# One mixture-of-experts kernel: thirteen larger experts do gate and up with the weights standing on the array, and the last expert's blocks go together

## The chip, the cores and the metric

The kernel runs on one core of one Trainium2 chip. The time is device microseconds (us) from the first to the last instruction of one launch, plus what little lies around it; the median of several launches counts. Engines are called by their short names: PE (matrix products), ACT (activations and copies), DVE (vector operations), POOL (here mostly indirect transfers), SP (issues the plain transfers). PEclk in the rows is the share of its full clock that PE was granted.

## The reference, cut to what matters

One layer on a sequence of tokens of 1,024 features: a normalised mLSTM branch and a pooling branch, an output product, and then a hierarchical mixture of 32 experts, each with gate, up and down matrices of 1024x512, 1024x512 and 512x1024. Each token goes to two experts; the last step is a norm over the whole output. The change is in the mixture and in the last norm.

```python
g_idx = argmax(hf @ w_rg + b_rg)                 # one of 4 groups
top_val, top_loc = lax.top_k(e_logits_of_that_group, 2)
gates = softmax(top_val) * g_gate
# for every expert e, over the tokens routed to it:
a = xb @ w_gate[e]
b = xb @ w_up[e]
out = (silu(a) * b) @ w_down[e]
y[token] += out * gate
x = x + gate_f * y
return rms_norm(x, final_g)
```

## The kernel before, in words

**Order of experts.** The experts are counted, ranked by size and taken in 32 positions (the loop variable `e`). Position 31, the last, holds the largest expert. Positions 3, 7 and 11 hold ranks 1 to 3; 13, 15, 17, 19, 21, 23, 25, 27 and 29 hold ranks 4 to 12. All other positions hold small experts of at most 128 tokens. So from position 12 on the positions alternate: an even one with one block of 128 rows (a single expert), an odd one with a larger expert.

**Products.** Everything is float32 in three passes: each operand is split into a high and a low part (`ehi`, `elo` for weights, `xh`, `xl` for the tokens), and a product is hi*xh + hi*xl + lo*xh. The weights of one expert come in 12 pieces of 128x1024; for each, ACT makes `ehi` (L143) and DVE makes `elo` (L144), one expert ahead of its use. The generator `feed` hands out these splits, and `take(n)` at named places (the hooks "gate", "silu", "up0", ...) puts n pieces into the instruction streams there. The engines work in the order in which the program is written.

**A single expert** (`core`, class `Block`). The tokens' rows are fetched by an indirect transfer on POOL (`gather`, tile `xg`, from `h2d`), turned by PE (`pxt`), split into `xh` and `xl`, and stand on the array; the weights stream through: 24 matmuls of 512 columns for gate (`pg`), 48 of 256 columns for up (`pu`), then 4 transposes of the activation (`pat`) and 24 matmuls of 512 columns for down (`py`). DVE weighs the result into `y` (L326) and POOL adds it to `acc` in DRAM with an indirect transfer (L334), one after the other.

**A larger expert** (`joint_core`). At ranks 1 to 3 it does two whole blocks, at ranks 4 to 12 one block and one half block of 64 rows (class `Half`), whose `xh` and `xl` stand side by side on the array, so that it needs two passes instead of three. In both, tokens stand and weights stream.

**Buffers.** The half block's turned activation `ahl` lies in the buffer `wraw1`, which the gather of the next larger expert's second block also uses: that gather waits for the last down product that reads `ahl`. `y` of a single and the first block's `y` share one buffer (tag `y`), which comes free when the scatter has landed.

**The last expert** (position 31). Its three blocks go one after the other (`core` for two, and for the third `half_core` or `core`, by a branch on the count). While they run, hooks fetch the 16 row tiles of `acc` (SP, L1749), square them on ACT (L1756), take the roots on DVE (L1760 and L135 to L139) and scale them on DVE (L1768) or on ACT and POOL (L1765, L1766).

Of the kernel before, what the change touches and what calls it, by code (L numbers as in the profile page):

```python
# [18 lines left out]
P = 128  # L19
T = 2048  # L20
# [19 lines left out]
SR = P // 2  # L40
N_FULL, N_HALF = 4, 9
# [12 lines left out]
def body(ctx, tc, x, c, ada_w, ada_b, norm1_g, w_in, conv_w, conv_b, w_q, w_k, b_igate, b_fgate,  # L54
# [46 lines left out]
    def full_at(q):  # L101
        return q == 0 or rank_at[q] < N_FULL

    def half_at(q):
        return N_FULL <= rank_at[q] < N_FULL + N_HALF
# [17 lines left out]
    cnt_p = const.tile([1, NE], I32, name="cnt_p")  # L123
# [23 lines left out]
    class Tiles:  # L147
# [5 lines left out]
        of_tag.update({t: 1 for t in ("xh", "xl", "act", "ah", "al", *(f"{a}2{q}" for a in ("ehi", "elo") for q in range(4)))})  # L153
# [70 lines left out]
    def gather(e, b, n=P):  # L224
        if e >= NE:
            return

        xg = xgs[e, 1] if b == 2 else hx.tile([P, D], F32, name="xg", tag=f"wraw{b}") if e or b else \
            wb.tile([P, D], F32, name="xg", tag="elo03")
        r = T if e or b else T - CH  # L230
        at = bass.IndirectOffsetOnAxis(ap=at_of(gix, gix_0, e, b)[0:n], axis=0)
        gathers.append(keep(G.indirect_dma_start(out=xg[0:n], out_offset=None, in_=h2d[0:r, :], bounds_check=r - 1,  # L232
                                                 oob_is_err=False, in_offset=at)))
        xgs[e, b] = xg

    def gather_further(e):

        if e < NE and full_at(e):
            gather(e, 1)
        elif e < NE and half_at(e):  # L240
            gather(e, 1, SR)

    def x_t(e, b):
        xg = xgs[e, b]
        n = "" if b == 0 else "i"
        xh = wb.tile([P, KT, P], F32R, name="xh" + n, bufs=1)
        xl = wb.tile([P, KT, P], F32R, name="xl" + n, bufs=1)
# [23 lines left out]
    class Block:  # L271


        def __init__(self, e, b, x, beside=False):
            self.e, self.b, self.x = e, b, x
            self.n = "i" if beside else ""
            self.pg = None

            self.y = wb.tile([P, D], F32, name="y", tag="yi") if beside else None
            self.a = self.y[:, 512:1024] if beside else wb.tile([P, DE], F32, name="act")  # L280
            self.ah = wb.tile([P, 4, P], F32R, name="ah", tag="ah" + self.n)
            self.al = wb.tile([P, 4, P], F32R, name="al", tag="al" + self.n)
            self.pus, self.py = {}, {}

        def turn_x(self, i):
            if i == 0:
                self.x = x_t(self.e, self.b)

        def gate(self, k0=0, k1=KT):
            if k0 == 0:  # L290
                self.pg = ps.tile([P, DE], F32, name="pg", tag="py0" if self.n else "pg", bufs=1)
            mm_all(self.pg, *self.x, lambda k: [t_[:, k % 2, :] for t_ in units[self.e, 0, k // 2]], k0, k1)
# [4 lines left out]
        def up(self, h, k0=0, k1=KT):  # L297
            if k0 == 0:
                self.pus[h] = ps.tile([P, 256], F32, name="pu", bufs=2)
            cs = slice(h * 256, h * 256 + 256)  # L300
            mm_all(self.pus[h], *self.x, lambda k: [t_[:, k % 2, cs] for t_ in units[self.e, 1, k // 2]], k0, k1)

        def gated(self, h):
            cs = slice(h * 256, h * 256 + 256)
            keep(V.tensor_tensor(self.a[:, cs], self.a[:, cs], self.pus[h], op=OP.mult))

        def turn(self, h):
            p_ = ps.tile([P, 2, P], F32, name="pat", bufs=1)
# [13 lines left out]
        def weigh(self, hf):  # L322
            if self.y is None:
                self.y = wb.tile([P, D], F32, name="y", tag="y" if self.e or self.b else "xh")
# [12 lines left out]
    class Half:  # L337
# [3 lines left out]
        def __init__(self, e, b, at, within):  # L341
            self.e, self.b, self.at, self.within = e, b, at, within
            self.xs = wb.tile([P, KT, P], F32R, name="xs", tag="xhi", bufs=1)
            self.y = wb.tile([SR, D], F32, name="ys", tag="xli", bufs=1)

            self.a = self.y[:, 512:1024]
            self.pus, self.py, self.as_ = {}, {}, None

        def turn_x(self, i):
            p_ = ps.tile([P, 4, SR], F32, name="pxs", tag="pxt", bufs=2)  # L350
            for j in range(4):
                PE.transpose(p_[:, j, :], xgs[self.e, self.b][0:SR, i * 4 + j::KT], ident[0:SR, 0:SR])
            s = slice(i * 4, i * 4 + 4)
            keep(S.activation(self.xs[:, s, 0:SR], p_, AF.Copy))
            keep(V.tensor_tensor(self.xs[:, s, SR:P], p_, self.xs[:, s, 0:SR].bitcast(F32), op=OP.subtract))

        def mm2(self, out_, a, bh, bl, first, last):
            PE.matmul(out_, a, bh, start=first, stop=False)
            PE.matmul(out_, a, bl, start=False, stop=last)

        def added(self, out_, p_):

            keep(S.activation(out_, p_[SR:P, :], AF.Copy))
            keep(V.tensor_tensor(out_, p_[0:SR, :], out_, op=OP.add))

        def gate(self):
            self.pg = ps.tile([P, DE], F32, name="pgs", tag="py0", bufs=1)
            for k in range(KT):
                hi, lo = units[self.e, 0, k // 2]
                self.mm2(self.pg, self.xs[:, k, :], hi[:, k % 2, :], lo[:, k % 2, :], k == 0, k == KT - 1)  # L370

        def silu(self):
            for h in range(2):
                cs = slice(h * 256, h * 256 + 256)
                self.added(self.a[:, cs], self.pg[:, cs])
            for h in range(2):
                cs = slice(h * 256, h * 256 + 256)
                keep(S.activation(self.a[:, cs], self.a[:, cs], AF.Silu))

        def up(self, h, k0=0, k1=KT):  # L380
            if k0 == 0:
                self.pus[h] = ps.tile([P, 256], F32, name="pu", bufs=2)
            cs = slice(h * 256, h * 256 + 256)
            for k in range(k0, k1):
                hi, lo = units[self.e, 1, k // 2]
                self.mm2(self.pus[h], self.xs[:, k, :], hi[:, k % 2, cs], lo[:, k % 2, cs], k == 0, k == KT - 1)

        def gated(self, h):
            cs = slice(h * 256, h * 256 + 256)
            t_ = self.y[:, cs]  # L390
            self.added(t_, self.pus[h])
            keep(V.tensor_tensor(self.a[:, cs], self.a[:, cs], t_, op=OP.mult))

        def turn(self, h):
            if self.as_ is None:
                self.as_ = wb.tile([P, 4, P], F32R, name="ahl", tag="ah", bufs=1) if self.within else \
                    hx.tile([P, 4, P], F32R, name="ahl", tag="wraw1")
            p_ = ps.tile([P, 2, SR], F32, name="pas", tag="pat", bufs=1)
            for j in range(2):
                PE.transpose(p_[:, j, :], self.a[:, (2 * h + j) * P:(2 * h + j + 1) * P], ident[0:SR, 0:SR])  # L400
            s = slice(2 * h, 2 * h + 2)
            keep(S.activation(self.as_[:, s, 0:SR], p_, AF.Copy))
            keep(V.tensor_tensor(self.as_[:, s, SR:P], p_, self.as_[:, s, 0:SR].bitcast(F32), op=OP.subtract))

        def down(self, k, hf):
            if hf not in self.py:
                self.py[hf] = ps.tile([P, 512], F32, name="pys", tag=f"py{hf}", bufs=1)
            hi, lo = units[self.e, 2, k]
            cs = slice(hf * 512, hf * 512 + 512)
            self.mm2(self.py[hf], self.as_[:, k, :], hi[:, 0, cs], lo[:, 0, cs], k == 0, k == 3)  # L410

        def weigh(self, hf):
            cs = slice(hf * 512, hf * 512 + 512)
            self.added(self.y[:, cs], self.py[hf])
            keep(V.scalar_tensor_tensor(self.y[:, cs], self.y[:, cs], gts[self.b][0:SR, self.e:self.e + 1],
                                        gate_f[0:SR, cs], op0=OP.mult, op1=OP.mult))

        def add(self):
            keep(G.indirect_dma_start(out=acc[:, :], in_=self.y, in_offset=None, bounds_check=T - 1, oob_is_err=False,
                                      out_offset=bass.IndirectOffsetOnAxis(ap=self.at[0:SR, self.e:self.e + 1], axis=0),  # L420
                                      compute_op=OP.add))

    def core(e, b, x, after=lambda m: None):
# [7 lines left out]
        A.gated(0)  # L431
# [4 lines left out]
        A.gated(1)  # L436
# [13 lines left out]
        if e < NE - 1:  # L450
            A.add()
        return A.y

    def half_core(e, b, after=lambda m: None):
        H = Half(e, b, six[b], True)
        for i in range(2):
            H.turn_x(i)
        H.gate()
        after("silu")
        H.silu()  # L460
# [1627 lines left out]
```

## Time and profile before

| | |
|---|---|
| time, median of 3 launches | 1662.3 us (1659.3 to 1669.67) |
| the profiled execution | 1654.61 us, span 1652.9 us |
| mean granted PE clock over the span | 0.978 |
| PE busy | 1558.2 us, 94% |
| DVE busy | 1381.8 us, 84% |
| ACT busy | 931.6 us, 56% |
| POOL busy | 272.9 us, 17% |

The profile is one execution. "Busy" counts an engine as busy from an instruction's start to its modelled end, so matmuls that overlap show longer ends than their spacing; the spacing of starts is what a stream of matmuls costs. The experts take the second half of the span, from 822 us on.

### The profile page before, as it was taken

How to read it: one execution, taken by the hardware profiler on the slowest of the kernel's cores; microseconds unless marked ns; L12 is line 12 of the kernel's file. 1: busy time of each engine (PE TensorE's matmuls, PEld its weight loads, DVE VectorE, ACT ScalarE, POOL GpSimd, SP SyncE). 2: the span in 40 equal slices, each digit the busy share in tenths (PEclk: the TensorE clock that was granted, in tenths of full speed). 3: DMA queues.
4: the chain of work that ended last, by engine and by line, in shares of the span. 5: the costliest groups of instructions: out<-in, count | busy, mean ns of one | idle time of the engine just before them, and what ended most of it. 6: DMA issues, size and time to landing. Idle time of an engine off the chain costs nothing. (4 is left out here: it accounts for less than half of the span.)

```text
span 1652.9 us, 25544 instructions
## 1 busy us (share of the span) xinstructions
PE 1558.2 (94%) x8865; PEld 1327.9 (80%) x8865; DVE 1381.8 (84%) x2754; ACT 931.6 (56%) x1501; POOL 272.9 (17%) x172
## 2 busy tenths in 40 slices
PE   3989999999999999999799999999999999999984
PEld 3868887877978788877688888888888888888873
DVE  6889877997789779988877887968889888899867
ACT  4246554655365554655366665746666666666653
POOL 0000000003020001000233331322123222132134
PEclk7999999999999999999999999999999999999997
DMA  8973276323652345345779898988898888898684
GB/s 306 320 253 103 81 240 202 126 63 105 240 113 76 103 153 159 85 155 197 266 249 358 297 383 269 390 262 283 306 338 292 292 283 294 309 337 314 222 294 198
DMA packets 143463, 384.94 MB, mean 233 GB/s; under 512 B 17220, under 2 KB 68459, under 8 KB 126942
## 3 DMA queue, kind: packets, MB, share of 16 engines
q1 hardware_dynamic: 124374, 340.95, 57.9%
q0 software_dynamic: 13920, 40.79, 9.8%
q10 hardware_dynamic: 5032, 1.51, 0.4%
q8 instruction: 71, 1.16, 0.3%
q14 instruction: 66, 0.54, 0.1%
HBM read 340.61 MB, written 48.08 MB: 235 GB/s over the span
## 5 line engine op out<-in xcount | busy, mean ns | idle before, releaser
L144 DVE TENSOR_TENSOR elo<-eraw,ehi 128x1024 fp32r<-128x1024 f32 x384 | 452.9, 1215 | 33.8 <-ACT ehi L143 26.5
L143 ACT ACTIVATE ehi<-eraw 128x1024 fp32r<-128x1024 f32 x384 | 382.1, 1054 | 19.4 <-PE py L260 7.8
L143 ACT ACTIVATE whi<-wraw 128x1024 fp32r<-128x1024 f32 (+1 forms) x100 | 105.8, 1058 | 146.0 <-PE big L260 52.4
L258 PE MATMUL big<-hh,whi 128*128 128x512 f32 x384 | 157.9, 411 | 0.7 <-DVE v L854 0.7
L260 PE MATMUL big<-hh,wlo 128*128 128x512 f32 x384 | 153.0, 399 | 2.0 <-DVE wlo L144 2.0
L259 PE MATMUL big<-hl,whi 128*128 128x512 f32 x384 | 153.7, 400 | 0.0
L334 POOL DMA_INDIRECT acc<-y,six x35 | 119.6, 3418 | 166.7 <-DVE y L326 141.5
L144 DVE TENSOR_TENSOR wlo<-wraw,whi 128x1024 fp32r<-128x1024 f32 (+1 forms) x100 | 122.2, 1222 | 20.4 <-ACT whi L143 19.1
L266 PE MATMUL pu<-ehi,xh 128*128 128x256 f32 x496 | 125.1, 286 | 0.0
L232 POOL DMA_INDIRECT xg<-h2d,gix x47 | 62.6, 1331 | 375.1 <-PE pxt L251 295.7
L267 PE MATMUL pu<-ehi,xl 128*128 128x256 f32 x496 | 123.8, 284 | 0.0
L258 PE MATMUL py<-ehi,ah 128*128 128x512 f32 x288 | 118.3, 411 | 4.1 <-ACT ah L312 4.1
L259 PE MATMUL py<-elo,ah 128*128 128x512 f32 x288 | 113.4, 394 | 0.0
L260 PE MATMUL py<-ehi,al 128*128 128x512 f32 x288 | 113.2, 395 | 0.0
L260 PE MATMUL big<-whi,yl 128*128 128x512 f32 x256 | 100.6, 408 | 8.0 <-DVE yl L144 7.8
L258 PE MATMUL big<-whi,yh 128*128 128x512 f32 x256 | 105.5, 413 | 1.4 <-ACT yh L143 1.2
L259 PE MATMUL big<-wlo,yh 128*128 128x512 f32 x256 | 102.3, 400 | 0.0
L266 PE MATMUL pg<-ehi,xh 128*128 128x512 f32 x248 | 98.2, 396 | 0.0
L1349 POOL DMA_INDIRECT table<-pay,si x28 | 37.2, 1329 | 363.2 <-DVE si L1344 210.8
L267 PE MATMUL pg<-ehi,xl 128*128 128x512 f32 x248 | 96.8, 390 | 0.0
L267 PEld LDWEIGHTS pu<-ehi,xl 128*128 128x128 f32 x496 | 94.9, 191 | 1.2
L266 PEld LDWEIGHTS pu<-ehi,xh 128*128 128x128 f32 x496 | 94.8, 191 | 1.3
(489 smaller groups left out, 3908.1 us busy)
## 6 DMA issues: line engine op xcount, KB each, us to landing
eraw<-in_w_expert_gate_dram SPq DMA_DIRECT2D x64, 1024.0 KB
eraw<-in_w_expert_up_dram SPq DMA_DIRECT2D x64, 1024.0 KB
eraw<-in_w_expert_down_dram SPq DMA_DIRECT2D x128, 512.0 KB, 7.4
wraw<-in_w_in_dram SPq DMA_DIRECT2D x64, 512.0 KB, 3.7
adaw<-in_ada_w_dram SPq DMA_DIRECT2D x40, 512.0 KB, 4.5
wraw<-in_w_out_dram SPq DMA_DIRECT2D x36, 512.0 KB, 4.1
xq<-in_x_dram SPq DMA_DIRECT2D x16, 512.0 KB, 6.3
bcs<-mad SPq DMA_DIRECT2D x16, 512.0 KB, 6.2
```

Source lines behind the costliest of these rows:

```text
L143: i = S.activation(hi, src, AF.Copy)
L144: j = V.tensor_tensor(lo, src, hi.bitcast(F32), op=OP.subtract)
L232: gathers.append(keep(G.indirect_dma_start(out=xg[0:n], out_offset=None, in_=h2d[0:r, :], bounds_check=r - 1, oob_is_err=False, in_offset= ...
L258: PE.matmul(out_, ah, bh, start=first, stop=False)
L259: PE.matmul(out_, ah, bl, start=False, stop=False)
L260: PE.matmul(out_, al, bh, start=False, stop=last)
L266: PE.matmul(out_, xh[:, k, :], hi, start=k == 0, stop=False)
L267: PE.matmul(out_, xl[:, k, :], hi, start=False, stop=False)
L334: keep(G.indirect_dma_start(out=acc[:, :], in_=self.y, in_offset=None, bounds_check=T - 1, oob_is_err=False, out_offset=at, compute_op=OP. ...
L1349: st = G.indirect_dma_start(out=table[:, :], out_offset=bass.IndirectOffsetOnAxis(ap=si[:, i, t:t + 1], axis=0), in_=pay[:, t, i, :], in_o ...
```

## The change

The class `Half`, `half_core`, `joint_core` and the branch at the end go. A class `Wide` takes their place at 13 positions, with as many rows as a table gives for each rank: 288 for the last position, 224 at ranks 1 to 3, 176 at ranks 4 to 7, 160 at 8 to 10 and 144 at 11 and 12. All R rows are one moving operand: a block of 128 weight columns stands on the array and [xh|xl] (2R columns) streams past its high part, xh (R columns) past its low part. A stage is 16 matmuls of 2R and 16 of R columns, and there are four (gate in two halves, up in two halves). The result comes out turned, so that the transposes of the activation fall away; the two halves of the R columns are added by an ACT copy and a DVE addition (methods `silu` and `gated`), in the buffers of `y`. The down product keeps its form: 24 matmuls for the first 128 rows, 16 or 24 for the rest (`pyb`). With 288 rows the operands are too wide for one bank, and xh and xl go one after the other.

```diff
-SR = P // 2
-N_FULL, N_HALF = 4, 9
+
+WIDE = (288, 224, 224, 224, 176, 176, 176, 176, 160, 160, 160, 144, 144)
...
+    class Wide:
...
+            for tag, k0, n in (("xw", 0, 4), ("xhl", 4, 4)) if self.both else (("xw", 0, 3), ("xhl", 3, 3), ("h", 6, 2)):
...
+                for b, r0, r in self.blocks:
+                    p_ = ps.tile([P, 4, P], F32, name="pxt", tag="pxt", bufs=2)
+                    for j in range(n):
+                        PE.transpose(p_[:, j, 0:r], xgs[e, b][0:r, k0 + j::KT], ident[0:r, 0:r])
...
+            if self.both:
+                self.ya[0] = wb.tile([P, D], F32, name="y")
+                self.ya[1] = wb.tile([P, D], F32, name="y", tag="yi")
+                self.act = self.ya[1][:, 0:4 * R].rearrange("p (i r) -> p i r", r=R)
+                self.sum = self.ya[0][:, 0:2 * R].rearrange("p (i r) -> p i r", r=R)
...
+                for k, i in steps[:-2]:
+                    mm(0, k, i, both[k], 2 * R, first=k == 0)
+                for k, i in steps:
+                    mm(1, k, i, self.xs[k][:, 0, :], R)
+                for k, i in steps[-2:]:
+                    mm(0, k, i, both[k], 2 * R, last=True)
...
+        def gated(self, p):
+            R, g, a = self.R, self.ps[1, p], self.act[:, 2 * p:2 * p + 2, :]
+            up = g[:, :, 0:R]
+            if self.both:
+                keep(S.activation(self.sum, g[:, :, R:2 * R], AF.Copy))
+                keep(V.tensor_tensor(self.sum, up, self.sum, op=OP.add))
+                up = self.sum
+            keep(V.tensor_tensor(a, a, up, op=OP.mult))
...
+    def wide_core(A, after):
+        A.begin()
+        A.stage(0, 0)
+        A.silu(0)
+        after("gate")
+        A.stage(0, 1)
+        A.silu(1)
...
+        A.stage(1, 0)
+        A.gated(0)
...
+        A.stage(1, 1)
+        A.gated(1)
+        for b in range(2):
+            for hf in range(2):
+                A.down(b, (0, 1), hf)
         after("turn")
...
+            A.down(0, (2, 3), hf)
+            A.weigh(0, hf)
+        A.add(0)
         after("down")
         for hf in range(2):
...
+            A.down(1, (2, 3), hf)
+            A.weigh(1, hf)
+        A.add(1)
+        after("end")
...
-                    nxt.append(x_t(e + 1, 0))
+                    nxt.append(Wide(e + 1) if wide_at(e + 1) else x_t(e + 1, 0))
...
+            for q in range(1, NE):
+                keep(V.memset(lim[:, q:q + 1], float(cap_at(q))))
...
+        def norm_rows(i):
+
+            ss = cm.tile([P, 4], F32, name="ssf", bufs=2)
+            for j in range(4):
+                square(rows_[i + j], ss[:, j:j + 1])
+            rs = roots(ss, 4, f"rsf{i // 4 % 2}")
+            for j in range(4):
+                scaled(rows_[i + j], rs[:, j:j + 1])
+                SP.dma_start(o2[(i + j) * P:(i + j + 1) * P, :], rows_[i + j])
...
+            norm_rows(0)
+            A.stage(1, 0)
+            A.gated(0)
+            norm_rows(4)
+            A.stage(1, 1)
+            A.gated(1)
```

The rest of the new last expert (`last_core`) fetches its own rows of `acc` again, multiplies down for the third, first and second block with `norm_rows(8)` and `norm_rows(12)` between them, adds, norms and stores the three blocks. All tensor operations of the last norm but the squares are on DVE now.

**On PE** the tokens of the next expert are turned inside the expert before it. Before, the half block's 64 rows (`pxs`) were turned in the middle of the larger expert's own gate; here the stream is at positions 12 and 13 (`pg` is gate, `py` down, `pxt` the first block's turn):

```order
L251 MATMUL pxt<-ident,xg 128x128 x8
...
L260 MATMUL py_12327<-ehi,al 128x512
L266 MATMUL pg<-ehi,xh 128x512
L267 MATMUL pg<-ehi,xl 128x512
...
L269 MATMUL pg<-elo,xh 128x512 x4
L352 MATMUL pxs<-ident,xg 128x64 x8
L266 MATMUL pg<-ehi,xh 128x512
```

Now, at position 20 with position 21's tokens coming, four of the last down products of position 19's second block (`pyb`) stand behind 14 gate matmuls of position 20, and the second block's turn (128x32) stands in the single expert's up, with half of `pu` behind it:

```order
L455 MATMUL pyb<-elo,ahl 112x512
L264 MATMUL pg<-ehi,x 128x512
...
L265 MATMUL pg<-ehi,x 128x512
L454 MATMUL pyb<-ehi,ahl 112x512
L455 MATMUL pyb<-elo,ahl 112x512
...
L267 MATMUL pg<-elo,x 128x512 x8
...
L267 MATMUL pu<-elo,x 128x256 x8
L354 MATMUL pxt<-ident,xg 128x128 x4
L354 MATMUL pxt<-ident,xg 128x32 x4
L264 MATMUL pu<-ehi,x 128x256
```

So 18 matmuls of 512 columns come ahead of the release of `wraw1`, and the turn of the rows that are fetched into `wraw1` comes 10 more of 512, 24 of 256 columns and 4 transposes later.

**On DVE** at the start of a single expert behind a larger one, before (`ys` is the half block's result, `act` the single's first half of silu(gate)*up):

```order
L364 TENSOR_TENSOR ys<-pys,ys 64x512
L415 SCALAR_TENSOR_TENSOR ys<-ys,slots,gate_f 64x512
...
L144 TENSOR_TENSOR elo<-eraw,ehi 128x1024 x6
L305 TENSOR_TENSOR act<-act,pu 128x256
L144 TENSOR_TENSOR elo<-eraw,ehi 128x1024
L313 TENSOR_TENSOR al<-pat,ah 128x256
```

and now:

```order
L466 TENSOR_TENSOR y<-pyb,y 32x512
L468 SCALAR_TENSOR_TENSOR y<-y,slots,gate_f 32x512
...
L143 TENSOR_TENSOR elo<-eraw,ehi 128x1024 x7
L302 TENSOR_TENSOR act<-act,pu 128x256
L143 TENSOR_TENSOR elo<-eraw,ehi 128x1024
L310 TENSOR_TENSOR al<-pg,ah 128x256
```

There is one split more ahead of the first `act`, and what stands ahead of the splits waits for `pyb`, whose second half is in the single's gate.

## Rows read from the trace of the kernel before

**Rows 1.** positions 13 and 14: length, busy us per engine, PEclk, DMA share, GB/s
```profile
1121.96:1171.56 49.60, 49.60 (x294) 43.09 (x293) 42.63 (x59) 32.27 (x47) 11.48 (x6) 1.00 0.87 303
```

**Rows 2.** timeline of PE, positions 3, 13, 14: start us, length, instruction
```profile
885.97 0.39 PE L266 MATMUL pg<-ehi,xh 128*128 128x512 f32 x1
...
909.76 0.40 PE L258 MATMUL py<-ehi,ah 128*128 128x512 f32 x1
...
1121.96 0.39 PE L266 MATMUL pg<-ehi,xh 128*128 128x512 f32 x1
...
1142.33 0.40 PE L258 MATMUL py<-ehi,ah 128*128 128x512 f32 x1
...
1153.40 0.40 PE L266 MATMUL pg<-ehi,xh 128*128 128x512 f32 x1
...
1156.62 0.39 PE L266 MATMUL pg<-ehi,xh 128*128 128x512 f32 x1
...
1158.88 0.28 PE L266 MATMUL pu<-ehi,xh 128*128 128x256 f32 x1
...
1160.67 0.28 PE L267 MATMUL pu<-ehi,xl 128*128 128x256 f32 x1
```

**Rows 3.** timeline of PE in the input product, where weights stand
```profile
639.78 0.39 PE L258 MATMUL big<-hh,whi 128*128 128x512 f32 x1
...
642.05 0.39 PE L259 MATMUL big<-hl,whi 128*128 128x512 f32 x1
```

**Rows 4.** tile pxs, position 13: ns min/median/max, first and last start
```profile
L352 PE MATMUL pxs<-ident,xg x8: 270/271/321, 1124.8 to 1125.6; 64*128 64x64 f32 x8
```

**Rows 5.** line L1220, the router's plain float32 product of 72 columns
```profile
L1220 PE MATMUL sm<-wr,x1T x32: 274/275/276, 795.8 to 799.2; 128*128 128x72 f32 x32
```

**Rows 6.** gathers of tokens (line L232, all 47)
```profile
DMA to landing us min/median/max: 4.2/8.6/10.7
```

**Rows 7.** the two gathers from 1153 to 1173 us (tile xg)
```profile
DMA to landing us min/median/max: 9.0/9.2/9.3
```

**Rows 8.** timeline of POOL, positions 13 and 14
```profile
1125.10 3.46 POOL L334 DMA_INDIRECT acc<-y,six  x1 [5.78 <-DVE y L326]
...
1154.35 1.00 POOL L232 DMA_INDIRECT xg<-h2d,gix  x1 [1.15 <-ACT ys L363]
```

**Rows 9.** scatters of y into acc (line L334, all 35)
```profile
DMA to landing us min/median/max: 6.8/11.0/16.6
```

**Rows 10.** timeline of DVE, position 14
```profile
1155.62 4.61 DVE L144 TENSOR_TENSOR elo<-eraw,ehi 128x1024 fp32r<-128x1024 f32 x4
...
1162.99 0.41 DVE L305 TENSOR_TENSOR act<-act,pu 128x256 f32<-128x256 f32 x1
```

**Rows 11.** groups of DVE by shape, 1122 to 1171.6 us: busy us, mean ns
```profile
L415 DVE SCALAR_TENSOR_TENSOR ys<-ys,slots,gate_f 64x512 f32<-64x512 f32 x2 | 1.5, 744 | 0.1
L364 DVE TENSOR_TENSOR ys<-pys,ys 64x512 f32<-64x512 f32 x2 | 1.4, 680 | 0.0
```

**Rows 12.** timeline of PE, position 31, behind a gap [idle, releaser]
```profile
1604.20 0.51 PE L258 MATMUL py<-ehi,ah 128*128 128x512 f32 x1 [3.60 <-ACT ah L312]
```

**Rows 13.** stretches of position 31, columns as in the first group
```profile
1599.96:1604.20 4.24, 0.64 (x6) 0.44 (x5) 1.96 (x6) 4.13 (x9) 0.23 (x1) 1.00 1.03 416
1604.60:1607.90 3.30, 3.30 (x11) 2.56 (x10) 3.21 (x5) 1.38 (x3) 3.30 (x2) 0.53 0.89 312
```

**Rows 14.** timelines of SP, ACT, DVE and POOL, position 31
```profile
1578.40 13.97 SPq L1749 DMA_DIRECT2D xf<-acc  x14
...
1583.33 1.06 ACT L1756 ACTIVATE jf<-xf 128x1024 bf16<-128x1024 f32 x1
...
1598.59 0.16 DVE L1760 TENSOR_SCALAR ssf<-ssf 128x4 f32<-128x4 f32 x1
...
1600.77 1.28 DVE L1768 SCALAR_TENSOR_TENSOR xf<-xf,rsf,fg 128x1024 f32<-128x1024 f32 x1
...
1647.61 0.97 POOL L1800 DMA_INDIRECT out_dram<-xa,six  x1 [4.08 <-DVE xa L1768]
```

More of the change, by code (lines that the diff above doesn't have):

```diff
@@ L236, in gather_further @@
     def gather_further(e):
[L238 to L241, printed above, removed]
+        for r0 in range(P, cap_at(e) if e < NE else 0, P):
+            gather(e, r0 // P, min(P, cap_at(e) - r0))
     def x_t(e, b):
[L244 to L247, printed above, removed]
+        x = wb.tile([P, 2, KT, P], F32R, name="x", tag="xw" if b else "xhl")
+        xg, xh, xl = xgs[e, b], x[:, 0], x[:, 1]
         for q in range(2):
@@ L449, in core @@
             A.weigh(hf)
[L450 to L458, printed above, removed]
+        A.add()
+    def wide_core(A, after):
[5 more added lines that the diff above has]
+        A.silu(1)
         after("silu")
-        H.silu()
-        H.up(0)
-        H.gated(0)
+        A.stage(1, 0)
+        A.gated(0)
@@ L1828, in last_hook, with last_core @@
+        def last_core(A, after):
+            e, n = A.e, [b[2] for b in A.blocks]
+            A.begin()
+            for _ in range(2):
                 t_ = hx.tile([P, 2, D], F32, name="xf", tag="h", bufs=4)
@@ new lines, in added, with store @@
+            def added(b, hf):
+                cs = slice(hf * 512, hf * 512 + 512)
+                A.weigh(b, hf)
+                keep(V.tensor_tensor(again[b][:, cs], again[b][:, cs], A.ya[b][0:n[b], cs], op=OP.add))
+            stored = []
+            def store(b):
+                stored.append(keep(G.indirect_dma_start(
+                    out=o2, out_offset=bass.IndirectOffsetOnAxis(ap=six[b][0:n[b], e:e + 1], axis=0), in_=again[b],
+                    in_offset=None, bounds_check=T - 1, oob_is_err=False)))
+                for i in stored[:-1]:
+                    tc.declare_no_dep(stored[-1].ins, i.ins, reason="an expert has a token once")
@@ new lines, in last_core @@
+            square(again[0], ss[:, 0:1])
+            A.down(1, range(4), 0)
+            A.down(1, range(4), 1)
+            rs = roots(ss, 2, "rsa")
+            for b, i in ((2, 1), (0, 0)):
+                scaled(again[b], rs[:, i:i + 1])
+                store(b)
+            ss = cm.tile([P, 2], F32, name="ssb")
+            for hf in range(2):
+                added(1, hf)
+                square(again[1][:, hf * 512:hf * 512 + 512], ss[:, hf:hf + 1])
+            keep(V.tensor_tensor(ss[:, 0:1], ss[:, 0:1], ss[:, 1:2], op=OP.add))
@@ L1844, in body @@
+            rs = roots(ss[:, 0:1], 1, "rsb")
+            scaled(again[1], rs)
+            store(1)
         x1 = [x_t(0, 1)]
```

482 lines of the change are left out of this document (186 added, 296 removed).

## The prediction

> **What bounds the kernel now.** I read the table of busy times first: PE is busy for 94% of the span, so PE's stream of matmuls sets the time as long as nothing makes it wait. Then I cut the expert part into stretches. In positions 13 and 14, one larger and one single expert, PE is busy for all of 49.60 us, DVE for 42.63, and the transfers fill 0.87 of the time, which is 43.2 us [rows 1]. So PE is the bound there, and two others are 6 to 7 us behind it in each such pair; from position 13 to 30 there are nine pairs. A change that takes PE work out of a pair gains until DVE or a transfer comes late. The timeline of PE gives what a matmul costs, by the spacing of starts and not by its length: 14 matmuls of 512 columns take 3.22 us (0.230 each), 15 of 256 columns 1.79 us (0.119 each) [rows 2]. With the weights standing, ten of 512 columns take 2.27 us [rows 3], so which side stands makes no difference in itself.
>
> **What the change removes from PE.** In position 13 the time from the first gate matmul to the first down matmul is 1142.33 - 1121.96 = 20.4 us [rows 2]: block and half block, with the turn of the half block's tokens inside. Four transposes of the half block's activation come later; with them it is about 20.9. In position 3, with two whole blocks, it is 23.8 us, with the transposes behind it 24.1 [rows 2].
>
> **What it adds on PE.** No matmul that streams fewer than 256 columns through this three-pass split stands in the trace. Between 256 and 512 columns the price is 0.119 + 0.434 ns for each further column. Below that, eight transposes of 64 columns start 0.114 us apart [rows 4] and 32 plain float32 products of 72 columns 3.4/31 = 0.110 us apart [rows 5]: so there is a floor of 0.11 us, for which the columns do not count. I take 0.111 us for the matmuls of R columns (144 to 224), since both rows are nearest in kind, and 0.133, 0.147, 0.161 and 0.202 us for those of 288, 320, 352 and 448. The ends: by columns alone 0.07 to 0.105 us, and if the plain product's 0.110 us were all due to its 72 columns (1.53 ns each), 0.22 to 0.34 us. The Trainium skill ("TensorE: Matmul & The Clock Gate", section "LDWEIGHTS (loading the stationary operand)") says that loading weights takes as long as there are weight columns, P/1.2 ns, 107 ns for 128, whatever is then streamed: that speaks against short streams past ever new weights, and rows 4 and 5 agree with it. By the columns alone, as if loading were free, each wider expert would give back some 1 to 2.5 us more.
>
> A stage is 16 of the wide and 16 of the narrow: 16 x (0.161 + 0.111) = 4.35 us at 176 rows, 4.13 at 160, 3.90 at 144, 5.01 at 224. Four of them and eight short transposes (0.9 us, as for `pxs`) make 18.3, 17.4, 16.5 and 20.9 us. Against 20.9 and 24.1 that saves 2.6 us at each of the four positions of 176, 3.5 at the three of 160, 4.4 at the two of 144 and 3.2 at the three of 224: 10.4 + 10.5 + 8.8 + 9.6 = **39 us** of PE, 2.4% of the time. Down keeps its matmuls.
>
> **What it makes wait: the second block's rows.** In each of the ten singles ahead of a larger expert (12, 14, ..., 30) the gather of that expert's second block needs the buffer that the last `pyb` product still reads. Counted from the single's first gate matmul (G), that product ends now behind 18 matmuls of 512 columns, at G + 4.1 us. Before, the gather started at 1154.35, G + 0.95 [rows 8], and was waited for only inside the next expert. A gather lands 8.6 us after its start in the median [rows 6]; the two of this stretch took 9.0 and 9.3 [rows 7]. So the rows are there at G + 12.7 to G + 13.4. But their turn stands in the single's up: PE is there after 28 x 0.230 + 24 x 0.119 + 4 x 0.111 = G + 9.7 us, and half of `pu` is queued behind it. PE waits **3.0 to 3.7 us**. With the fastest gather of all (4.2 us) it would wait for nothing here, with the slowest (10.7) 5.1.
>
> **What it makes wait: DVE.** In the same singles DVE's additions and weighings of `pyb`'s second half wait for those same products. They are ready at G + 4.1, an ACT copy (0.6, as long as DVE's copies of this shape), 0.68 and 0.74 us on DVE end at G + 6.1 [rows 11], seven splits at 4.61/4 = 1.15 us follow [rows 10], and `act` (0.41) is done at G + 14.6. Before, six splits ended so that `act` started at 1162.99, G + 9.6 [rows 10]. PE wants `act` about 1.9 us after the turn of the tokens (12 `pu` matmuls and four transposes), which is G + 11.6 if it waited for nothing: 3.0 us late as well. The two waits overlap, since PE stands at the turn anyway. Either is enough for about 3 us; I count 3.3 once. At the two positions behind 224 rows whose next larger expert is far off (4 and 8) only DVE's part is there; there the single's PE stream is later by 24 rather than 16 `pyb` products, and I count 1.25.
>
> **The clock.** On position 31 PE stood idle for 3.60 us [rows 12]; before that stretch it had run at a granted 1.00, and in the 3.3 us behind the gap it got 0.53, its lower level of 1.2 GHz [rows 13]. Half of 3.3 us is 1.65 us of work that is done later. No gap stands in the steady pairs now, and their PEclk is 1.00 [rows 1]. With a gap of 3.0 to 3.7 us in each of ten singles I count 1.65 us for each: 16.5 us. Nothing excludes that the clock holds in some; the ends are 0 and twice that. The Trainium skill (the same page, section "HAM oscillation — how this bites in real kernels") tells of a kernel whose PE waits for a transfer in every step and starts every step at the lower clock; rows 12 and 13 show one such gap, and by that rule the 16.5 us are due, without it none.
>
> **What else waits.** `gated(0)` of a larger expert writes into the `y` of the single before it, and so waits until that scatter has landed. With W the larger expert's first gate matmul: the scatter started at 1125.10, W + 3.1 [rows 8], comes about 1 us later with two more token tiles on DVE ahead of it, and lands 11.0 us later [rows 9], at W + 15.1. Two copies, three DVE operations follow, about 2 us (0.4 each by shape), to W + 17.1. PE's four stages end at W + 17.4, 16.5 and 15.6 for 176, 160 and 144 rows: nothing, 0.6 and 1.5 us of waiting, about 0.55 us as a mean over the nine. Thirty-one one-element fills on DVE in position 0 and the list operations that are emptied at position 28 cost up to 2 us each; I take 2 for both, and 0 and 4 as ends.
>
> **The last expert.** PE's part there shrinks from three blocks one after the other to one pass, but the end is set elsewhere. Now it starts at 1568.70 (nine pairs behind 1121.96) and ends 84.2 us later. `acc`'s rows still wait for the last scatter, with nine token tiles on DVE ahead of its `y`; SP's fetches started at 1578.40 and ACT's first square at 1583.33, 14.6 us in [rows 14]; I shift them by 4.5 us to 19.1. Four squares at 1.2 us, roots from 1598.59 to 1600.77 (2.2 us), four scalings at 1.22 us [rows 14]: one group of four is 12 us, and the groups follow in series, since the squares of the next stand on ACT behind copies that wait for a DVE product behind the scalings. The first scalings end 32 us in; two more serial groups with `gated` end at 46 and 60; the third and first block's additions, the fourth group, whose squares are hidden, and the additions between make 72; two squares, roots, two scalings, the second block's additions, its square, roots and scaling 87. The store is then 5.3 us from the end, as at 1647.61 [rows 14]. That is 92 us, **8 more** than now; if the squares do not block, two times 5 us less, 2 fewer than now. I take +6.
>
> **The sum.** Nine pairs: -29.7 (savings at 176, 160 and 144) + 9 x 3.3 + 9 x 1.65 + 9 x 0.55 = +19.8. Positions 11 and 12: -3.2 + 3.3 + 1.65 = +1.8. Positions 3 and 7: 2 x (-3.2 + 1.25) = -3.9. Small things +2, the end +6. Together **+26 us**. The profiled execution is 1654.6 us, 0.5% under the median of the runs, 1662.3; carried over to the median, **1688 us**, 1.6% slower. The terms that are unsure: the waits (3.0 to 3.7 in ten singles, +-4 in all), the end (-8 to +2), the floor.
>
> **The rivals.**
>
> *The waits come, the clock holds.* Gaps of 3 us that leave the clock at 1.00 take 16.5 us out: +10, 1672 us, no change that can be told. For it: the gap is overlapped by nothing else, but it lies close to the shortest gaps; against it rows 12 and 13. A little shorter waits, by gathers that land in 7 us in a stretch with fewer bytes, lead the same way.
>
> *PE's saving comes through.* If the gathers land within 5.6 us of their start and DVE reaches `act` by G + 11.6, nothing waits: -39 + 2 + 6 = -31, 1631 us, 1.9% faster. Against it: DVE's 42.63 us a pair do not shrink, and at a pair of 46.3 us it would have to be busy for over 92% with no waits of its own; and most gathers take 8.6 us.
>
> *Narrow streams cost more.* If a product of fewer than 256 columns costs 1.53 ns a column, the 64 narrow ones of each larger expert cost 64 x (0.343 - 0.111) = 14.8 us more at 224 rows, 10.1 at 176, 8.6 at 160 and 7.0 at 144: +125, about 1813 us. Only rows 5 would allow it, and the 64-column transposes, at the same spacing, speak against it.
>
> **How the numbers follow.** Forecast 0.49, clock holds 0.30, saving comes through 0.15, narrow streams 0.06. A measurement of this kernel can tell about 1% from no change, 17 us. Faster by over 1% is most of the third, 0.13; slower is nearly all of the forecast, the upper edge of the second and the fourth, 0.56; the rest is 0.31. The forecast's own range is 1674 to 1704 by its unsure terms; the second reaches from 1650 to 1682. The range that leaves out the other two is 1650 to 1705.
>
> **What would show it.** In the changed profile: PE's busy share well below 94% although no stage is longer than above; in the singles 14 to 30 a PE gap of 3 us or more ahead of `pxt` of 16 to 48 columns, ended by the gather or at the next turn by DVE's `act`; PEclk under 1.00 in the same slices; single stretches of some 24 us (from 18) and larger ones of 26 to 27 (from 31); the narrow matmuls 0.11 us apart; and the last part 90 us or longer with DVE as its chain. What would make it wrong: gathers that start before the last `pyb` product or land in 5 us, DVE ahead of its splits, a clock of 1.00 behind the gaps.

## The result and the profile after

The changed kernel takes 1739.78 us in the median (1734.38 to 1743.28, 4 runs) against 1660.94 us of the kernel before beside it: a ratio of 1.0461, 95% interval 1.0412 to 1.0509, or 79 us slower. Run a second time among the experiments, it took 1731.15 us and gave a ratio of 1.0443 (1.0394 to 1.0493). The forecast was 1688 us with a range of 1650 to 1705, and the time lies above it.

The profiled execution has a span of 1740.3 us, 87.4 more than the profiled one before. Cut into four parts, the experts show where this arose. Before the gate of position 1 are 7.9 us, of which 5.3 lie ahead of the first token turn of the experts, in code that both kernels share; the second run of the same kernel has 2 there, so this part is no sign of the change. From position 1 to position 13 are 23.1 us (forecast -2), from 13 to 31 44.9 (forecast +20), and in the last expert 11.5 (forecast +6).

First the stretches, with the columns of [rows 1]: a larger expert's four stages (position 15, 176 rows), and behind the mark the larger expert 13 (144 rows), the single 14, the wait in it, the stretch behind the wait, and position 31 to the end.

```profile
1209.17:1226.58 17.41, 17.41 (x129) 17.41 (x128) 13.77 (x19) 10.56 (x16) 2.57 (x2) 1.00 0.88 284
...
1152.97:1182.84 29.87, 27.94 (x173) 24.43 (x172) 21.45 (x35) 16.54 (x25) 3.62 (x3) 0.89 0.74 244
1182.84:1209.17 26.33, 22.14 (x122) 19.14 (x120) 20.34 (x25) 14.69 (x21) 10.40 (x4) 0.94 0.86 287
1192.13:1197.58 5.45, 1.25 (x10) 0.94 (x9) 5.45 (x7) 3.80 (x5) 4.04 (x1) 0.98 0.97 372
1197.70:1200.30 2.60, 2.60 (x12) 2.60 (x13) 0.96 (x1) 0.00 (x0) 2.17 (x1) 0.50 1.04 416
1644.61:1740.30 95.69, 46.33 (x266) 39.54 (x264) 57.24 (x123) 33.37 (x62) 9.36 (x7) 0.75 0.52 202
```

The four stages take 17.41 us, as forecast (17.4). A single, 18.2 us before by the starts in [rows 2] (1153.40 to position 15's gate at 1171.56), takes 26.33. In the 5.45 us from 1192.13 PE is busy for 1.25 and DVE for all of it; in the 2.60 us behind, PE works at half its clock.

What PE waited for from 830 us on (the view of waits: us in total, times, longest):

```profile
PE pu L264 <- DVE act L302: 49.0, 18, 7.0
PE pxt L354 <- DMA xg<-h2d,gix: 20.0, 10, 10.5
PE py L256 <- ACT ah L420: 9.9, 5, 6.8
...
PE pyb L454 <- DVE y L466: 2.5, 3, 1.7
```

The gather is second, and more than half of its 20.0 us is one wait of 10.5 in position 12. The third is `ah`, the high part of the activation, for the down product; 6.8 of its 9.9 us is one wait in position 31. First is a wait that the forecast did not have in this place: `pu`, the second half of up, for `act`. The timelines of PE and of DVE in position 14 (the gate starts at 1182.84 = G; the brackets give the idle time before and what ended it):

```profile
1193.60 0.64 PE L354 MATMUL pxt<-ident,xg 48*128 48x48 f32 x4 [0.85 <-DMA xg<-h2d,gix]
1197.58 0.58 PE L264 MATMUL pu<-ehi,x 128*128 128x256 f32 x1 [3.34 <-DVE act L302]
```

```profile
1187.79 0.68 DVE L466 TENSOR_TENSOR y<-pyb,y 16x512 f32<-16x512 f32 x1 [1.29 <-ACT y L465]
1188.51 0.74 DVE L468 SCALAR_TENSOR_TENSOR y<-y,slots,gate_f 16x512 f32<-16x512 f32 x1
1189.18 8.02 DVE L143 TENSOR_TENSOR elo<-eraw,ehi 128x1024 fp32r<-128x1024 f32 x7
1197.12 0.40 DVE L302 TENSOR_TENSOR act<-act,pu 128x256 f32<-128x256 f32 x1
```

DVE does what the forecast said, to 0.3 us: `y` done at G + 6.4, seven splits, `act` done at G + 14.7. But PE needed it at once, before a single matmul of the second half, and not at the later turn of `act`. The gather came 0.85 us late and no more. In position 6, a single with no larger expert ahead, the same wait stands:

```profile
981.74 0.39 PE L264 MATMUL pu<-ehi,x 128*128 128x256 f32 x1 [1.40 <-DVE act L302]
```

The cause is in `Block.up`. PE writes its products into tiles of PSUM, and both halves of up are now slices of one such tile `pu` (`self.u[:, h, 0:256]`), though in two banks of it (the tile is `[P, 2, 512]`, and each `[P, 512]` of it is a bank). DVE's product of the first half reads that tile, and PE's first write into it for the second half waits for this read. Before, `pu` was two tiles. The second block's down product has the same form: both halves of `pyb` are one tile, the second half's last products wait for DVE's addition of the first (the last row of the waits), and in the stream they stand behind 14 matmuls of the next gate.

Last the price of narrow matmuls, which no row of before had for this product, in position 15:

```profile
1211.42 1.92 PE L381 MATMUL pgu<-x,elo 128*128 128x176 f32 x16
1213.17 2.76 PE L381 MATMUL pgu<-x,ehi 128*128 128x352 f32 x16
1215.77 1.92 PE L381 MATMUL pgu<-x,elo 128*128 128x176 f32 x16
```

Sixteen of 176 columns take 1.75 us by the starts (0.109 each), sixteen of 352 take 2.60 (0.163).

### The profile page after: what moved, and what is told of

It reads as the page before. It is cut to its first block, busy times and chain, and to the rows that moved or that the text cites. A ratio compares the mean times of both kernels' runs of the same rounds, so it can differ in the third digit from the quotient of the medians.

```text
span 1740.3 us, 25273 instructions
## 1 busy us (share of the span) xinstructions
PE 1552.6 (89%) x8781; PEld 1334.4 (77%) x8781; DVE 1380.3 (79%) x2793; ACT 920.3 (53%) x1496; POOL 298.1 (17%) x165
## 5 line engine op out<-in xcount | busy, mean ns | idle before, releaser
L234 POOL DMA_INDIRECT xg<-h2d,gix x47 | 81.8, 1740 | 431.6 <-PE pxt L249 212.4
L381 PE MATMUL pgu<-x,ehi 128*128 128x288 f32 (+3 forms) x896 | 155.2, 323 | 0.0
L381 PEld LDWEIGHTS pgu<-x,ehi 128*128 128x128 f32 x896 | 139.8, 188 | 3.8
L264 PE MATMUL pu<-ehi,x 128*128 128x256 f32 x304 | 94.4, 337 | 49.2 <-DVE act L302 49.0
L256 PE MATMUL py<-ehi,ah 128*128 128x512 f32 x256 | 106.6, 416 | 9.9 <-ACT ah L420 9.9
L264 PEld LDWEIGHTS pu<-ehi,x 128*128 128x128 f32 x304 | 69.7, 229 | 52.9 <-DVE act L302 51.8
L258 PE MATMUL py<-ehi,al 128*128 128x512 f32 x256 | 101.7, 398 | 0.0
L381 PE MATMUL pgu<-x,elo 128*128 128x176 f32 (+4 forms) x832 | 101.3, 274 | 0.0
L381 PEld LDWEIGHTS pgu<-x,elo 128*128 128x128 f32 x832 | 100.4, 191 | 0.4
L331 POOL DMA_INDIRECT acc<-y,six x20 | 69.5, 3475 | 131.3 <-DVE y L323 97.9
```

The lines of the kernel that those rows point to most:

```text
L256: PE.matmul(out_, ah, bh, start=first, stop=False)
L258: PE.matmul(out_, al, bh, start=False, stop=last)
L264: PE.matmul(out_, xh[:, k, :], hi, start=k == 0, stop=False)
L381: PE.matmul(g[:, i, 0:n], w, x, start=first, stop=last)
```

## The experiments

Ratios are to launches of the kernel before that were measured beside the run, with a 95% interval; the changed kernel itself stands at 1.046 and 1.044. Each edit is to the changed kernel, unless it says that it goes on top of others.

**The halves of up apart.** The half products get a tile each; the first borrows the bank of `py0`, which is free then.

```diff
-                self.u = self.u or ps.tile([P, 2, 512], F32, name="pu", tag="gu", bufs=2)
-                self.pu = self.u[:, h, 0:256]
+                if k0 == 0:
+                    self.pu = ps.tile([P, 512], F32, name="pu", tag="py0", bufs=1)[:, 0:256] if h == 0 else \
+                        ps.tile([P, 2, 512], F32, name="pu", tag="gu", bufs=2)[:, 1, 0:256]
```

> The changed kernel with one edit: the first half of a single expert's up product gets a PSUM bank of its own (that of the first down product), so that the two halves no longer share one tile. Theory of the shared tile (PE waits at the second half of up until DVE has read the first half of the same tile): the waits of PE for act at that place (49.0 us, 18 times) go; the twelve singles that follow no larger expert lose 1.5 us each, the ten that follow one lose about 3 of their 4.6 us and the half clock behind it (1.5 us): 18 + 44 = 62 us less, about 1678 us. Theory of the late gather (the prediction's first wait): the gap stays, ended by the gather; at most 15 us less, 1725 us. If DVE as a whole is the bound, act is as late as before and the wait only moves to its turn: 1725 us or more.

1702.86 us, ratio 1.0279 (1.0245 to 1.0314): by the ratios 27 to 30 us less than the changed kernel, half of what the theory of the shared tile gave, and more than the others allow. The wait of `pu` for `act` is gone; what is left of it stands at the turn of `act`, and the list of waits begins

```profile
PE pg L308 <- DVE act L303: 18.9, 9, 5.2
PE py L256 <- ACT ah L421: 11.5, 5, 6.8
PE pxt L355 <- DMA xg<-h2d,gix: 6.8, 1, 6.8
```

From position 1 to 13 PE waits for `act` nowhere any more. The pair of positions 15 and 16 is still 51.70 us. `pyb` still stands behind the 14 gate matmuls here, DVE's queue still begins with it, and the row shows the wait for the addition of the first half:

```profile
1215.82 0.49 PE L455 MATMUL pyb<-ehi,ahl 128*112 128x512 f32 x1 [0.38 <-DVE y L467]
```

**The gather's own buffer** (the prediction's first wait).

```diff
-        if b == 2:
+        if b == 2 or b == 1 and 0 < e < NE - 1:
             xg = wb.tile([P, D], F32, name="xg", tag="xf")
```

> The changed kernel with one edit: the gather of a larger expert's second block goes into a buffer of its own, so that it no longer waits for the last down product of the larger expert before. Late gather: the waits at the turn of these rows are what costs, 33 us of waits and up to 16 us of lower clock come back, 1690 to 1707 us. Shared tile and DVE's queue: PE waits for act all the same, only the wait of position 12 (10.5 us) can go, 1728 to 1740 us.

1734.05 us, 1.0462 (1.0433 to 1.0491): no change that can be told, as the theory of the shared tile had it. The waits for the gather fall from 20.0 to 1.4 us and those for `act` grow from 49.0 to 60.1. In its profile positions 11 and 12 take 54.2 us where the changed kernel takes 64.8. The late gather is real, and apart from that one place PE waits in its stead for `act`.

**Two splits behind up instead of ahead of `act`.**

```diff
-                    take(2 if e else 0)
+                    take(2 if wide else 0)
...
                 elif m == "up1":
-                    take(2)
+                    take(4 if e else 2)
```

> The changed kernel with one edit: in single experts the two weight splits of the hook behind gate are handed out behind up instead, so two of the seven splits of DVE stand behind act's first half and no longer ahead of it. Shared tile with DVE's queue: act comes 2.3 us earlier in 22 singles, 1.5 us of wait goes in each of twelve and 2.3 us, with some of the lower clock, in each of ten: 1685 to 1700 us. Late gather: nothing changes, 1735 to 1745 us. If the splits are late for the next expert instead, new waits for elo appear in the larger experts and the time stays or grows.

1722.62 us, 1.0386 (1.0359 to 1.0414): 9 to 12 us less, so DVE's queue takes part, by less than expected. The waits for `act` fall to 22.8 us, but PE now waits 17.3 us in 18 places for `al`, the low part of the activation, which stands behind the moved splits on DVE, and 12.8 for the gather.

**The last expert's squares one group earlier.**

```diff
+            norm_squares(0)
+            norm_squares(4)
             norm_rows(0)
             A.stage(1, 0)
             A.gated(0)
+            norm_squares(8)
             norm_rows(4)
             A.stage(1, 1)
             A.gated(1)
+            norm_squares(12)
```

> The changed kernel with one edit in the last expert: the four squares of the next group of rows are issued on ACT ahead of the copies of gated instead of behind them. Serial groups (squares wait behind copies that wait for DVE): two times 5 us come back at the end, the stretch from position 31's first matmul falls from 95.7 to 86 us, 1730 us. DVE's own work bounds the end: 0 to 3 us, 1737 to 1740 us.

1720.12 us, 1.0382 (1.0340 to 1.0424), 10 to 13 us less. From position 31's first matmul behind the last turn of tokens to the end the changed kernel takes 92.30 us and this one 80.90, with the same busy times:

```profile
1648.00:1740.30 92.30, 42.94 (x243) 36.58 (x242) 55.21 (x118) 31.93 (x57) 9.36 (x7) 0.74 0.54 210
```

```profile
1637.50:1718.40 80.90, 42.91 (x243) 36.67 (x242) 54.95 (x118) 32.06 (x57) 11.05 (x7) 0.77 0.62 239
```

So the groups of squares were in series for the reason forecast.

**All two-bank tiles apart.** `pu`, `pyb`, a single's gate and the stages of the larger experts get one tile per bank (tag `gu`, four buffers instead of two of double size). No run has `pyb` alone apart.

```diff
-            g = self.ps[m, p] = ps.tile([P, 2, 512], F32, name="pgu", tag="gu", bufs=2)
+            g = self.ps[m, p] = [ps.tile([P, 512], F32, name="pgu", tag="gu", bufs=4) for _ in range(2)]
...
-                    t_ = ps.tile([P, 2, 512], F32, name="pyb", tag="gu", bufs=2)
-                    self.py[b, 0], self.py[b, 1] = t_[:, 0, :], t_[:, 1, :]
+                    self.py[b, hf] = ps.tile([P, 512], F32, name="pyb", tag="gu", bufs=4)
```

> The changed kernel with one edit: every PSUM tile of two banks becomes two tiles of one bank (the two halves of up, of a larger expert's stages, and of its second block's down product), at the price of four more ACT and four more DVE operations in each larger expert. Shared tile: both places where PE waits for DVE's read of the other half go, so the last down products stand ahead of the next gate, DVE's additions and its act come 3 us earlier, and a pair falls from 53.8 to 47 to 48 us; 75 us less, 1660 to 1672 us. If DVE's own work is what bounds (42 us busy in a pair), a pair stays near the 51.4 us of the run with the own bank for up, and the time near 1700 us.

1666.76 us, 1.0048 (1.0028 to 1.0067): 64 us less than the second run of the changed kernel. Pairs take 47.5 to 52.4 us, but 54.5 with position 28's list operations. The last `pyb` products now stand ahead of the next gate, and `act` of the single with its gate at 1195.31 starts at G + 12.9 instead of G + 14.3. Two pairs, from position 15 on, columns as in [rows 1]:

```profile
1167.40:1218.20 50.80, 49.20 (x293) 43.85 (x292) 42.19 (x61) 31.77 (x50) 13.75 (x7) 0.97 0.88 306
1218.20:1266.70 48.50, 46.06 (x294) 40.31 (x293) 41.55 (x61) 31.42 (x50) 14.72 (x7) 1.00 0.86 291
```

**With the gather's own buffer and the early squares.** The three edits together.

> As before, with the gather's own buffer and the early squares of the last expert as well. If the causes are separate, their gains add: 11 us at the end and little by the gather, 1648 to 1660 us, at or just under the kernel before. If the early squares gained only because PE was late, the end gains less than 5 us here.

1662.90 us, 1.0020 (0.9999 to 1.0040). The three together give 4 us more than the tiles alone, not 11. In the profiles the end does gain: from the same matmul of position 31 to the end of the span it takes 80.8 us (1580.3 to 1661.1) after 89.7 (1575.3 to 1665.0). But position 31 starts 5 us later: 1.2 us lie ahead of the experts, 1.5 in positions 0 to 12, and 1.9 in positions 13 and 14, where PE waits 1.43 us for `ah` instead of 0.50 and position 13 has a PEclk of 0.94 instead of 1.00.

**And with the sum in its own buffer and three list operations per expert.**

```diff
-                self.sum = self.ya[0][:, 0:2 * R].rearrange("p (i r) -> p i r", r=R)
+                self.sum = wb.tile([P, 512], F32, name="sum", tag="sum")[:, 0:2 * R].rearrange("p (i r) -> p i r", r=R)
...
-                    for _ in range(2 if e else 0):
+                    for _ in range(3 if e else 0):
```

> As the second, and the sum of a larger expert's up halves lies in a buffer of its own and not in y, and three list operations instead of two are done per expert, so that none are left to be emptied at position 28. The waits of PE for ah (10 us in 5 or 6 places) come from y's scatter: they go, and the pair behind position 28 loses its extra 4 us: 5 to 10 us less than the second. If those waits are DVE's, nothing changes.

1653.71 us, 0.9967 (0.9948 to 0.9986). The stretch from position 27's stages to those of 29, with position 28's list operations in it, falls from 54.8 to 49.0 us. The waits for `ah` do not go (12.5 us in 8 places after 10.7 in 6, with 7.3 and 6.4 of them in position 31): they do not come from `y`'s scatter, as the prediction had it. ACT's copy into `ah` waits for DVE's product, in position 15:

```profile
1193.28 0.42 ACT L425 ACTIVATE ah<-y 128x256 fp32r<-128x256 f32 x1 [2.19 <-DVE y L417]
```

**The changed kernel again.**

> The changed kernel once more, unchanged, beside the others on the same chip: 1725 to 1742 us. It says how much of the 20 us by the early squares and of the 6 us by the gather's own buffer is the edit and how much the chip or the launch.

1731.15 us, 1.0443 (1.0394 to 1.0493). The same kernel differs by some 8 us between two series of launches, so a difference of this size between series says nothing, and the readings here go by ratios.

**Splits between ACT's two steps, in the changed kernel.** In a larger expert ACT copies, DVE adds, ACT does silu; the splits of the hook are put between.

```diff
         A.silu(0)
         after("gate")
+        A.act_silu(0)
...
-        A.gated(0)
+        A.mult(0)
         after("up0")
+        A.split_act(0)
```

> The changed kernel with one edit in the larger experts: the weight splits of the hooks stand between ACT's copy of the low half and ACT's silu (and between the product and ACT's copies of it), so that ACT does not stand waiting for DVE's addition while DVE then waits for ACT's next split. Theory of the round trip (about 1.5 us of DVE idle, three times in each larger expert, which makes DVE's queue late in the single behind it): act comes earlier, 30 to 45 us less, about 1690 to 1700 us. Shared tile alone: DVE's idle time in the larger expert is slack that it gets back, and at most 10 us come back, 1722 to 1735 us.

1745.71 us, 1.0539 (1.0514 to 1.0565): no gain but 13 to 16 us slower, outside of what both theories gave. New waits of PE for `al` in the larger experts (6.4 us in 9 places) and longer ones for `ah` (12.8 us after 9.9) make up most of it. In its single behind position 15 (gate at 1228.16 = G) DVE stands idle and `act` starts at G + 14.3, as in the changed kernel:

```profile
1233.13 0.68 DVE L477 TENSOR_TENSOR y<-pyb,y 48x512 f32<-48x512 f32 x1 [1.31 <-ACT y L476]
...
1242.47 0.40 DVE L302 TENSOR_TENSOR act<-act,pu 128x256 f32<-128x256 f32 x1
```

So with the shared tile an earlier DVE gains nothing in the single: it waits there for ACT's copy of the second half of `pyb`.

**The same on top of all edits.**

> The kernel with all the edits of the run before last (own banks, own gather buffer, early squares, own sum, three list operations) and the splits between as well. Round trip: DVE's idle time of some 4 us in each larger expert goes, the waits for act and ah that are left (8 and 12 us) go with their clock, and pairs come near PE's own 46.6 us: 1625 to 1640 us. If DVE has no slack left at all, 1648 to 1655 us.

1639.54 us, 0.9904 (0.9875 to 0.9933). Without the shared tiles the same edit gives some 10 us by the ratios. The waits for `ah` in the larger experts are gone; the one that is left stands in position 31. This is the fastest of the versions that compute the whole, and about 1% faster than the kernel before.

**All edits with two splits later.**

> The same all-edits kernel with two splits of a single expert's hook moved behind up instead. The waits for act (8.1 us in ten places, with 0.75 us of lower clock each) go, those for ah in the larger experts (12.5 us) stay or grow: 1640 to 1652 us. If the queue of DVE only shifts, no gain: 1652 to 1660 us.

1654.20 us, 0.9987 (0.9972 to 1.0002): no gain over the all-edits kernel. The waits for `act` fall from 8.1 to 3.4 us, and those for `al` take their place (6.9).

**DVE relieved.**

> The all-edits kernel with every second low part of the weights left out (PE multiplies the high part in its place, so PE, ACT and the transfers do what they did; from position 2 on DVE has 14 us less work in a pair). DVE bounds what is left: pairs fall to PE's 46.6 us, 1620 to 1630 us. PE's own stream or the transfers bound it: pairs stay at 49 to 50 us, 1648 to 1655 us.

1618.17 us, 0.9769 (0.9746 to 0.9793). This kernel leaves out every second low part of the weights and so does not compute the layer; it only shows what PE's stream allows. Pairs fall to PE's own time; in the pairs from position 15 and 17 on PE is busy for all of it, while DVE is at 31 of 47 and 29 of 45 us:

```profile
1159.00:1206.10 47.10, 47.10 (x294) 42.83 (x293) 31.21 (x54) 31.91 (x50) 9.49 (x6) 1.00 0.87 306
1206.10:1251.40 45.30, 45.30 (x294) 40.21 (x293) 28.94 (x52) 31.96 (x50) 10.10 (x7) 1.00 0.93 334
```

The view of waits has none of PE from position 1 to 30, and one for `ah` in position 31, 3.8 us. So the saving on PE is there, and what keeps it from coming through once the tiles are apart is DVE's work and its order.

## Why the prediction was right and wrong

**PE's saving: right.** Four stages of 176 rows were put at 17.4 us and take 17.41; the narrow matmul's 0.111 us is 0.109. By the forecast's savings a pair without waits takes 49.6 - 2.6 = 47.0 us at 176 rows and 49.6 - 4.4 = 45.2 at 144; with DVE relieved it takes 47.10 and 45.30. The third rival, narrow streams that cost more, is refuted by these rows. The Trainium skill's rule ("TensorE: Matmul & The Clock Gate", section "LDWEIGHTS (loading the stationary operand)") of 107 ns for each load of 128 weight columns agrees with the 0.109.

**The wait for DVE: the step that failed.** The prediction put `act` at G + 14.6 (measured: done at G + 14.7) and then said that "PE wants `act` about 1.9 us after the turn of the tokens". It wants it before the second half of up, since both halves share a tile. That is 1.4 us earlier, so the second half of up in a single behind a larger expert starts 4.5 us late (5.45 with 0.9 of transposes) and not 3.3. And the wait stands in the singles that follow a single, too, with 0.6 to 1.7 us each, where the forecast had none. The prediction had looked for the matmuls that need the operand, and had not asked what the first matmul behind the turn must wait for. The run with the tiles of up apart takes 27 to 30 us off, that with `pyb` and all other two-bank tiles apart as well 64 to 71 of the 72 to 79; how much of the second step is `pyb` alone was not measured.

The waits of the singles and larger experts from position 13 to 30 were put at 29.7 and 5.0 us. The view of waits there:

```profile
PE pu L264 <- DVE act L302: 33.4, 9, 7.0
PE pxt L354 <- DMA xg<-h2d,gix: 9.5, 9, 1.5
PE py L256 <- ACT ah L420: 3.1, 4, 1.9
```

With 1.2 us for `y` that is 44 us in the singles and 3 in the larger experts. The part from position 1 to 13, where the forecast saw a gain of 2 us and 23 were lost, has 13.1 us of this wait for `act` in 8 places and the one late gather of 10.5.

**The late gather: right in kind, too large, and overlapped.** Forecast 3.0 to 3.7 us in ten singles. From 1153 us on the gathers land 5.4 us after their start in the median, and not 8.6 to 9.3 [rows 6, 7], though the one in position 14 starts at G + 5.1 and not G + 4.1; so PE waits 0.85 us there, and 0.7 to 1.5 in the nine singles from 14 to 30. The overlap with DVE's wait was foreseen ("Either is enough"), and a buffer of its own for the gather changes nothing that can be told.

**The clock: as forecast in kind, and too small.** A wait of 3.34 us behind one of 0.85 is followed by 2.60 us at a granted 0.50, the lower level of 1.2 GHz, as in [rows 12, 13]; the whole single 14 has 0.94. So the first rival, in which the clock holds, falls. The Trainium skill's section "HAM oscillation — how this bites in real kernels" of the same page describes this repeated fall, there behind waits for a transfer; here it comes in each single from 14 to 30. With two splits later one pair has 1.00 again. What the clock costs alone was not run apart, but the granted clock gives an estimate. Read in steps of 0.25 us between the gates of positions 1 and 31, PE is busy for 64 us at the lower level (52 in the second run), and for none before the change. There a matmul of 512 columns takes 0.43 us by the starts (position 13) instead of 0.23, so by this estimate some 30 us are lost (24 in the second run), and not the 16.5 that were forecast. Some of it stands where the forecast had no lower clock: behind a wait of 1.93 us for `ah` in position 13 come 6.6 us at a granted 0.51.

**`y`'s scatter: small and wrongly named.** 0.55 us a pair were put down to it, and the larger experts from 13 to 29 have 3.1 us in all. These waits for `ah` stay with the sum in its own buffer, and go when the splits stand between or DVE is relieved, so they come from the order and the length of DVE's queue.

**The list operations: mis-sized.** Forecast 2 us with the fills. The stretch from position 27 to 29 gets 5.8 us shorter when they are spread (with the sum's buffer in the same run).

**The end: right in kind, a little small.** Forecast +6 from a working of +8; it was +11.5, and 11.4 come back when the squares are early. With the tiles apart the end gains 8.9 us by it in the profiles, though the time of the three edits together gains only 4; why the other 5 are lost ahead of position 31 is open.

**The second rival, the saving coming through**, was given with a condition on DVE, over 92% busy with no waits of its own at a pair of 46.3 us. The last runs bear out that DVE decides: with the tiles apart and the splits between, one pair takes 46.30 us with DVE busy for 88% of it, and 16 to 17 us under the kernel before come through; with DVE relieved it is 38 to 39.

```profile
1211.50:1257.80 46.30, 45.69 (x293) 40.10 (x292) 40.93 (x63) 31.44 (x50) 12.87 (x7) 1.00 0.93 325
```

Open besides: why the gather of position 12 takes 10.22 us on POOL in the changed kernel and 0.93 into its own buffer. It is not alone: in positions 4 and 8, behind the other experts of 224 rows, a gather takes 10.28 and 10.29 us, but its rows are not needed there yet. With all two-bank tiles apart none of them takes over 2.1 us, so the time does not come from the shared buffer alone.

## What to carry to other kernels

When a change merges buffers, ask of each merged tile who reads its first half while the second half is written: here the engine that wrote waited for the reader of the other half, as a wait that had to be followed to its producer. A saving on the busiest engine is worth what the next engine's queue lets through; with DVE at 42 of 49.6 us nearly none of it came through until DVE's operands came early and its splits stood in its own waits, and a relieved DVE showed at once how much there was. Two waits in the same place hide each other: removing the late gather alone measured nothing, since PE then waited for `act` in its stead.

## What was not expected of the hardware

A gather of tokens landed 5.4 us after its start (4.3 to 6.2) from 1153 us on, where 9.0 to 9.3 had been read before [rows 7]: 5.0 to 6.2 us with 16 to 48 rows, 4.3 to 5.7 with the 128 of a first block. Before 1153 us three gathers landed only 15.7 to 17.7 us after their start, all behind experts of 224 rows.

Forecast from other shapes, but not seen in this product before: the price of a matmul with a freshly loaded block of 128 weight columns does not fall with the streamed columns from 224 down to 144. It is 0.111 or 0.112 us in the median at 144, 160, 176 and 224.
